# A 64x64 triangular inverse finished ahead of a four-group recurrence, one solve per group

## The chip, the cores and the metric

One core of one Trainium2 chip runs one program. The metric is the device time in microseconds (us) of one execution; the median of three runs of the kernel before is 899.11 us (898.23 to 902.22). Differences below 0.5% (4.5 us) count as no change.

## The reference

A trunk of two residual layers over 256 tokens of width 1024 in float32. The first layer adds an RWKV-7 time mixing and a retention to the residual, the second a differential attention; each layer then has a cross-attention into 256 memory tokens and a squared-ReLU MLP. Only the RWKV-7 scan matters here. It is, per head (8 heads of 64 channels) and per token t:

```
sa    = state @ a_t
state = state * w_t + sa (x) b_t + v_t (x) k_t
y_t   = state @ r_t
```

with `a = -kk`, `b = kk * a`, decays `w`, and a state of 64x64 that starts at zero. Its output goes through a group norm, a gate and an output projection.

## The kernel before, in words

The scan is computed in chunks: the 256 tokens are four groups g of 64 tokens. Group g lies in half `hf = g // 2` (a half is 128 tokens, one per partition) and in the partitions `gg` of half `gp = g % 2` (0 to 63 or 64 to 127). Within a group the dependence of a token on earlier ones is a strictly lower triangular 64x64 matrix per head, so the group needs the inverse of a unit triangular matrix. `inverse()` (L573) computes on the vector engine only the two 32x32 diagonal blocks of that inverse, for 8 heads x 4 groups at once, and leaves them in `X` (128 x 16 x 32). The block between them is never formed: it is applied inside the recurrence, in three steps per group, with `ga` the first 32 tokens of a group and `gb` the last 32.

One pass of the loop over g (L749 on) is a chain:

- for g > 0, `RS = AR^T S` (L757 on): the state `S` of the group before, 8 matmuls of 64x64, four heads at a time (`h2` is the half of the partitions, that is the rows of the array, which holds the head's channels), each four followed by an addition into the right side `LV` on the vector engine (L763)
- `solve(ga)` (L766): 8 matmuls 32x32 by 64 columns, `LV` with `X`, and two copies out of the bank to `U`, columns 0 to 255 on DVE (L770) and 256 to 511 on ACT (L771)
- `Q` (L774 on): 8 matmuls 32x32 by 64 columns, `U` of `ga` with the scores `SCb`, and an addition into `LV` of `gb` (L778)
- `solve(gb)`: as `solve(ga)`
- for g < 3 the new state: 8 matmuls `kT, vT` into KVp, 8 matmuls `bT, U` into Sp, and vector operations with the decay (L792 to L797)

After g = 2 `outputs(0)` (L692), after the loop `finish(0)` (L727) and `outputs(1)`: outputs of a half are 32 matmuls of 64x64 (`U, SCb` and `vT, SCk`), the same product of `AR` with the state (8 or 16 matmuls, `YS`, in fours by `h2`), a group norm (reductions on DVE, a square on ACT, a power on POOL), four transposes and the gate.

All matmuls are written out in order by the program, but which one TensorE runs when is set by a scheduler that takes the instructions by priority as their inputs come free. Behind the recurrence stand the projections of the memory tokens for the cross-attention (`kv_chunk`, matmuls of `memh` and `meml` with the weights `hi` and `lo`, 128x128 by 256 or 512 columns, called filler below); they need nothing of the recurrence, and the scheduler puts them between its steps. Each engine then runs its list in that order and waits where an input is missing.

Matmul outputs go to eight banks in three pools: `acc` (4), `mm` (2), `tr` (2). All steps of the recurrence took theirs from `tr` (`tr_t()`). A float32 matmul appears in the trace as two MATMUL rows and two LDWEIGHTS rows (8 matmuls of `solve` are 16 rows), a matmul on split weights as one. The helper `mm` (L121) records nearly all matmuls, so groups are told apart by their tiles: `tr<-LV,X` is a solve, `tr<-U,SCb` at 32*32 is Q, `tr<-S,AR` is RS or YS, `tr<-vT,kT` is KVp, `tr<-U,bT` is Sp, and `mm<-memh,hi` and its like are filler. In a row, 32*32 or 64*64 is the part of the array that is used.

Of the kernel before, what the change touches and what calls it, by code (L numbers as in the profile page):

```python
# [37 lines left out]
def kernel(ctx: ExitStack, tc: tile.TileContext, ins: dict, out: bass.AP):  # L38
    nc = tc.nc
# [6 lines left out]
    const = ctx.enter_context(tc.tile_pool(name="const", bufs=1))  # L46
# [25 lines left out]
    def acc_t():  # L72
        return ps_acc.tile([128, 512], F32, tag="acc", name=nm("acc"))
# [45 lines left out]
    def mm(o, lhsT, rhs, start, stop):  # L119

        ins = nc.tensor.matmul(o, lhsT=lhsT, rhs=rhs, start=start, stop=stop)  # L121
        key = o.tensor.name
        prev = last_in_bank.get(key)
        if prev is not None:
            behind(ins, prev, "one accumulation group per bank")
        last_in_bank[key] = ins
# [56 lines left out]
    def proj_rows(w, c0, xT, evac, alloc):  # L183

        xh, xl = xT
        ps = [alloc(), alloc()]
        for pc in range(4):
            wh, wl = wpiece(w[pc * 256:(pc + 1) * 256, c0:c0 + 512].rearrange("(kt p) c -> p kt c", p=128), 2, 512)
            for t in range(2):
                for k2 in range(2):  # L190
                    kt = 2 * pc + k2
                    mm3_x(ps[t], xh[:, kt, t * 128:(t + 1) * 128], xl[:, kt, t * 128:(t + 1) * 128],
                          wh[:, k2, :], wl[:, k2, :], kt == 0, kt == 7)
        for t in range(2):
            evac(ps[t], t)
# [163 lines left out]
    omu = const.tile([128, 14], F32, name="omu")  # L359
    behind(nc.vector.tensor_scalar(omu, prm[:, R_MU:R_MU + 14], -1.0, 1.0, op0=ALU.mult, op1=ALU.add), d1[1], "the activations first")  # L360
    oka = const.tile([128, 4], F32, name="oka")
    const.tile([128, 22], F32, name="pad")

    quad = const.tile([128, 2], F32, name="quad")
    for q in range(4):
# [166 lines left out]
    def rope_evac(i):  # L532
        def ev(ps, t):
            p4 = ps.rearrange("p (h x d) -> p h x d", h=8, x=2)
            cs, sn = rope_tabs(i, t)
            dst = qkR[i][:, t, :].rearrange("p (h x d) -> p h x d", h=8, x=2)
            tm = scratch()[:, :512].rearrange("p (h x d) -> p h x d", h=8, x=2)
            nc.vector.tensor_tensor(dst, p4, cs.unsqueeze(2).broadcast_to([128, 8, 2, 32]), op=ALU.mult)
            for x in range(2):
                nc.vector.scalar_tensor_tensor(tm[:, :, x, :], p4[:, :, 1 - x, :], 2.0 * x - 1.0, sn,  # L540
                                               op0=ALU.mult, op1=ALU.mult)
            nc.vector.tensor_tensor(dst, dst, tm, op=ALU.add)
        return ev
# [30 lines left out]
    def inverse():  # L574
# [21 lines left out]
        nc.vector.transpose(X.rearrange("p h (m par) -> p m par h", par=2), Xc.rearrange("p s m -> p m s"))  # L596
        Xt[0] = X

    proj_rows(wh_in, A_COLS + 512, xT, rope_evac(1), acc_t)
    proj_rows(wh_in, A_COLS, xT, rope_evac(0), acc_t)  # L600
    kTr = to_chan(1)
# [74 lines left out]
    def hidx(hd):  # L676
        return (hd % 2) * 4 + hd // 2
# [12 lines left out]
    ycs = {}  # L690

    def outputs(hf):  # L692
        Yp = tr_t()
        for hd in range(8):
            for gp in range(2):
                gg = slice(gp * 64, gp * 64 + 64)
                e = slice(hd * 64, hd * 64 + 64)
                mm(Yp[gg, e], lhsT=SCb[gg, hf, hidx(hd), 64:128], rhs=U[gg, hf, e], start=True, stop=False)
                mm(Yp[gg, e], lhsT=SCk[gg, hf, hidx(hd), 64:128], rhs=vT[gg, hf, e], start=False, stop=True)
        Y = pC.tile([128, 512], F32, tag="RH", name=nm("Y"))  # L700
        nc.scalar.activation(Y, Yp, AF.Copy)
        yg = slice(64, 128) if hf == 0 else slice(0, 128)
        for h2 in range(2):
            pr = slice(h2 * 64, h2 * 64 + 64)
            YS = tr_t()[:, :256].rearrange("p (b e) -> p b e", b=4)
            for gp in range(2):
                g = 2 * hf + gp
                gg = slice(gp * 64, gp * 64 + 64)
                if g > 0:
                    for b in range(4):  # L710
                        mm(YS[gg, b, :], lhsT=AR[pr, b * 4 + g, 1, :], rhs=Sv[g][pr, b, :], start=True, stop=True)
            yv = Y[yg, :].rearrange("p (b h e) -> p h b e", b=4, h=2)[:, h2]
            nc.vector.tensor_tensor(yv, YS[yg], yv, op=ALU.add)
        Y3 = Y.rearrange("p (h e) -> p h e", h=8)
        sm = small.tile([128, 8], F32, tag="sm8", name=nm("sm"))
        nc.vector.tensor_reduce(sm, Y3, axis=AX.X, op=ALU.add, negate=True)
        nc.vector.tensor_scalar(sm, sm, 1.0 / 64, None, op0=ALU.mult)
        yc = pC.tile([128, 8, 64], F32, tag="yc", name=nm("yc"), bufs=2)
        nc.vector.tensor_tensor(yc, Y3, sm.unsqueeze(2).broadcast_to([128, 8, 64]), op=ALU.add)
        sq = pC.tile([128, 8, 64], F32, tag="ysq", name=nm("ysq"))  # L720
        nc.scalar.activation(sq, yc, AF.Square)
        s2 = small.tile([128, 8], F32, tag="s28", name=nm("s2"))
        nc.vector.tensor_reduce(s2, sq, axis=AX.X, op=ALU.add)
        rs = rstd_of(s2, 64, 8, GN_EPS)
        nc.vector.tensor_tensor(yc, yc, rs.unsqueeze(2).broadcast_to([128, 8, 64]), op=ALU.mult)
        ycs[hf] = yc

    def finish(hf):
# [14 lines left out]
        nc.vector.tensor_tensor(ya, ya, pg2.rearrange("p (b t) -> p b t", b=4), op=ALU.mult)  # L743
        split(yT[0][:, 0:4, hf * 128:(hf + 1) * 128], yT[1][:, 0:4, hf * 128:(hf + 1) * 128], ya)


    U = pA.tile([128, 2, 512], F32, tag="bt", name="U")
    Sv = [None]
    for g in range(4):  # L749
        hf, gp = g // 2, g % 2  # L750
        ga = slice(gp * 64, gp * 64 + 32)
        gb = slice(gp * 64 + 32, gp * 64 + 64)
        gg = slice(gp * 64, gp * 64 + 64)
        S = Sv[g]
        RH = LV[:, hf, :]
        if g > 0:
            for h2 in range(2):  # L757
                RS = tr_t()[:, :256].rearrange("p (b e) -> p b e", b=4)
                pr = slice(h2 * 64, h2 * 64 + 64)
                for b in range(4):  # L760
                    mm(RS[gg, b, :], lhsT=AR[pr, b * 4 + g, 0, :], rhs=S[pr, b, :], start=True, stop=True)
                rv = RH[gg, :].rearrange("p (b h e) -> p h b e", b=4, h=2)[:, h2]
                nc.vector.tensor_tensor(rv, RS[gg], rv, op=ALU.add)  # L763
        Up = tr_t()

        def solve(prt):  # L766
            for hd in range(8):
                e = slice(hd * 64, hd * 64 + 64)
                mm(Up[prt, e], lhsT=Xt[0][prt, hf * 8 + hidx(hd), :], rhs=RH[prt, e], start=True, stop=True)
            nc.vector.tensor_copy(out=U[prt, hf, 0:256], in_=Up[prt, 0:256])  # L770
            nc.scalar.activation(U[prt, hf, 256:512], Up[prt, 256:512], AF.Copy)  # L771

        solve(ga)
        Q = tr_t()  # L774
        for hd in range(8):
            e = slice(hd * 64, hd * 64 + 64)
            mm(Q[gb, e], lhsT=SCb[ga, hf, hidx(hd), 32:64], rhs=U[ga, hf, e], start=True, stop=True)
        nc.vector.tensor_tensor(RH[gb, :], Q[gb, :], RH[gb, :], op=ALU.add)  # L778
        solve(gb)
        if g < 3:  # L780
            KVp, Sp = (tr_t()[:, :256].rearrange("p (b e) -> p b e", b=4) for _ in range(2))
            for tgt, lh, rh in ((KVp, kT, vT), (Sp, bT, U)):
                for hd in range(8):
                    b, h2 = hd // 2, hd % 2
                    e = slice(hd * 64, hd * 64 + 64)
                    mm(tgt[h2 * 64:h2 * 64 + 64, b, :], lhsT=lh[gg, hf, e], rhs=rh[gg, hf, e], start=True, stop=True)
            Sn = pC.tile([128, 4, 64], F32, tag="S", name=nm("S"), bufs=3)
            SP = pC.tile([128, 4, 64], F32, tag="SP", name=nm("SP"), bufs=1)

            pg = Ep.rearrange("p (b g) t -> p b g t", b=4)[:, :, g, 64:65]  # L790
            if g == 0:
                nc.vector.tensor_tensor(SP, KVp, pg.broadcast_to([128, 4, 64]), op=ALU.mult)  # L792
            else:
                nc.vector.tensor_tensor(SP, KVp, S, op=ALU.add)
                nc.vector.tensor_tensor(SP, SP, pg.broadcast_to([128, 4, 64]), op=ALU.mult)
            for b in range(4):
                nc.vector.scalar_tensor_tensor(Sn[:, b, :], Sp[:, b, :], pg[:, b, :], SP[:, b, :], op0=ALU.mult, op1=ALU.add)  # L797
            Sv.append(Sn)
        if g == 2:
            outputs(0)  # L800
# [505 lines left out]
```

## Time and profile before

| what | value |
|---|---|
| median of three runs | 899.11 us (898.23 to 902.22) |
| the profiled execution, device time | 897.66 us |
| its span in the profile | 895.9 us |
| PE busy (matmul) | 876.5 us, 98% |
| DVE, ACT busy | 593.5 us, 454.9 us |
| granted TensorE clock, mean | 0.995 |
| the recurrence with its outputs | about 153 to 214 us of the span |

The span is the time from the first to the last instruction; the device time is 1.8 us more. PE busy counts a matmul from its start to its modelled end, so rows of matmuls overlap; what a run of matmuls costs TensorE is read from the start of its first row to the start of the next work.

### The profile page before, as it was taken

The page shows a single profiled execution, that of the slowest core. Times are in us where ns is not written, and L with a number is a line of the kernel's source. Part 1 is how long each engine was busy: PE and PEld are TensorE (multiplying, and loading weights), DVE is VectorE, ACT ScalarE, POOL GpSimd, SP SyncE. Part 2 cuts the span into 40 slices and gives each one's busy share as a digit, 9 for nine tenths or more (in the row PEclk, how much of TensorE's full clock was granted, in tenths as well). Part 3 has the DMA queues.
Part 4 walks back from the last instruction along what each step waited for, and adds up shares of the span by engine and source line. Part 5 has one row for each costly group of instructions (what it writes and reads, how often), then busy time and mean ns, then how long its engine had stood idle before and what let it go on. Part 6 is the DMA issues. An engine that isn't in the chain of part 4 may idle for free.

```text
span 895.9 us, 14122 instructions
## 1 busy us (share of the span) xinstructions
PE 876.5 (98%) x5546; PEld 752.6 (84%) x5546; DVE 593.5 (66%) x937; ACT 454.9 (51%) x730; POOL 30.5 (3%) x51
## 2 busy tenths in 40 slices
PE   7999999999999999999999999999999999999996
PEld 5988889777889889888888889978899888888885
DVE  4669888455476557666666675786776676666665
ACT  5765444324465436444444454674564554444443
POOL 2000000001000100000000000001000000000001
PEclk8999999999999999999999999999999999999999
DMA  9754433222656545565555555443563465655551
GB/s 310 237 152 129 140 120 119 72 72 95 198 203 213 185 168 191 195 190 192 193 189 189 188 175 180 142 124 113 170 203 97 153 198 188 188 189 191 188 189 66
DMA packets 47078, 149.98 MB, mean 167 GB/s; under 512 B 4731, under 2 KB 4900, under 8 KB 46884
## 3 DMA queue, kind: packets, MB, share of 16 engines
q1 hardware_dynamic: 45456, 142.73, 49.2%
q10 hardware_dynamic: 1108, 3.72, 1.2%
q0 software_dynamic: 448, 2.63, 0.8%
q8 instruction: 43, 0.70, 0.3%
q14 instruction: 23, 0.19, 0.1%
HBM read 148.01 MB, written 2.63 MB: 168 GB/s over the span
## 4 chain that ended last, share of the span: by engine, by line
PE 90%; DVE 4%; issue 2%; ACT 2%; POOL 1%; DMA 1%; POOLq 0%; SPq 0%; DVEq 0%; ACTq 0%
PE mm L121 37%; PE acc L121 35%; PE tr L121 15%; DVE lo L129 1%; PE tr L254 1%; ACT hi L129 1%; DMA h<-in_x_dram 1%; PE tr L1111 1%; PE tr L958 1%; DVE z L1092 0%; PE acc L254 0%; POOL rs L226 0%; DVE xn L268 0%; PE tr L500 0%; POOL xn L1189 0%
## 5 line engine op out<-in xcount | busy, mean ns | idle before, releaser
L129 DVE TENSOR_TENSOR lo<-raw,hi 128x1024 fp32r<-128x1024 f32 x262 | 320.0, 1223 | 213.3 <-ACT hi L129 211.1
L129 ACT ACTIVATE hi<-raw 128x1024 fp32r<-128x1024 f32 x262 | 277.6, 1060 | 333.5 <-PE mm L121 122.5
L121 PE MATMUL mm<-xhl,hi 128*128 128x256 f32 (+1 forms) x784 | 188.0, 319 | 1.3 <-ACT xhl L129 1.1
L121 PEld LDWEIGHTS mm<-xhl,hi 128*128 128x128 f32 x784 | 129.7, 189 | 12.1 <-ACT xhl L129 2.0
L121 PE MATMUL mm<-xhl,lo 128*128 128x256 f32 x512 | 138.1, 282 | 0.0
L121 PE MATMUL acc<-hi,hl 128*128 128x512 f32 x256 | 100.2, 391 | 0.0
L121 PE MATMUL acc<-hi,hh 128*128 128x512 f32 x256 | 100.1, 391 | 0.0
L121 PE MATMUL acc<-lo,hh 128*128 128x512 f32 x256 | 99.6, 389 | 0.0
L121 PEld LDWEIGHTS mm<-xhl,lo 128*128 128x128 f32 x512 | 96.6, 189 | 2.5
L121 PE MATMUL tr<-xhl,hi 128*128 128x512 f32 x256 | 92.8, 395 | 0.0
L121 PE MATMUL acc<-hi,xhl 128*128 128x512 f32 x256 | 81.9, 396 | 0.0
L121 PE MATMUL tr<-xhl,lo 128*128 128x256 f32 x256 | 66.7, 281 | 0.0
L121 PEld LDWEIGHTS acc<-hi,hl 128*128 128x128 f32 x256 | 48.0, 188 | 11.3 <-DVE hl L129 0.9
L121 PEld LDWEIGHTS acc<-lo,hh 128*128 128x128 f32 x256 | 48.1, 188 | 10.4
L121 PEld LDWEIGHTS acc<-hi,xhl 128*128 128x128 f32 x256 | 47.7, 188 | 9.7
L121 PEld LDWEIGHTS acc<-hi,hh 128*128 128x128 f32 x256 | 48.1, 188 | 8.8
L121 PEld LDWEIGHTS tr<-xhl,hi 128*128 128x128 f32 x256 | 48.2, 188 | 8.5
L121 PEld LDWEIGHTS tr<-xhl,lo 128*128 128x128 f32 x256 | 48.2, 188 | 2.9
L121 PE MATMUL acc<-lo,xhl 128*128 128x512 f32 x128 | 50.4, 394 | 0.0
L121 PE MATMUL mm<-memh,hi 128*128 128x256 f32 x128 | 37.0, 289 | 0.0
L121 PE MATMUL mm<-meml,hi 128*128 128x256 f32 x128 | 36.8, 288 | 0.0
L121 PE MATMUL mm<-memh,lo 128*128 128x256 f32 x128 | 36.5, 285 | 0.0
(303 smaller groups left out, 1369.5 us busy)
## 6 DMA issues: line engine op xcount, KB each, us to landing
raw<-in_w_dram SPq DMA_DIRECT2D x64, 512.0 KB, 4.3
raw<-in_mlp_w_dram SPq DMA_DIRECT2D x64, 512.0 KB, 4.3
raw<-in_hyb_w_in_dram SPq DMA_DIRECT2D x16, 512.0 KB, 3.7
raw<-in_w_k_dram SPq DMA_DIRECT2D x16, 512.0 KB, 3.5
raw<-in_xattn_w_kv_dram SPq DMA_DIRECT2D x16, 512.0 KB, 3.7
raw<-in_w_q_dram SPq DMA_DIRECT2D x16, 512.0 KB, 4.0
raw<-in_xattn_w_o_dram SPq DMA_DIRECT2D x16, 512.0 KB, 3.5
raw<-in_w_dqk_dram SPq DMA_DIRECT2D x16, 512.0 KB, 3.6
```

What stands on the lines that cost most here:

```text
L121: ins = nc.tensor.matmul(o, lhsT=lhsT, rhs=rhs, start=start, stop=stop)
L129: return nc.scalar.activation(hi, src, AF.Copy), nc.vector.tensor_tensor(lo, src, r32(hi), op=ALU.subtract)
L254: nc.tensor.transpose(ps[:, k4, :], x[:, kt * 128:(kt + 1) * 128], ident)
L958: nc.tensor.transpose(pt[:, j, m, :], P[:, j, m * 128:(m + 1) * 128], ident)
L1111: nc.tensor.transpose(pt[:, k * 128:(k + 1) * 128], z3[:, 0, k * 128:(k + 1) * 128], ident)
```

## The change

The whole 64x64 inverse is formed once, ahead of the loop, by the new function `whole_inverse()`: `T` (128 x 16 x 64) gets the two diagonal blocks from `X`, and its third block from two sets of 32 matmuls of 32x32 by 32 columns (scores with the transposed blocks, then the result with the blocks). Two activations, one 32x32-block transpose on DVE, and four copies out of banks (two on ACT, two on DVE, by half of the partitions) go with it. In the loop `solve(ga)`, `Q` and `solve(gb)` become one solve: 8 matmuls of 64x64 by 64 columns, four heads into the partitions `gg` of one bank and four into the other partitions `og` of a second bank, in turn. RS and YS alternate the two row halves `h2`, with a bank for each. RS, the solve and the outputs take their banks from `acc` instead of `tr`.

```diff
+    def whole_inverse():
+
+        X = Xt[0]
+        T = pB.tile([128, 16, 64], F32, tag="Lc", name="T")
+        for j in range(2):
+            nc.scalar.activation(T[:, :, j * 32:j * 32 + 32], X, AF.Identity, scale=quad[:, j:j + 1])
+        Xn = pB.tile([128, 16, 32], F32, tag="Xc", name="Xn")
+        nc.vector.transpose(Xn.rearrange("p h t -> p (h t)"), X.rearrange("p h t -> p (h t)"))
+        Wt = pC.tile([128, 16, 32], F32, tag="ysq", name="Wt")
+        Wp, Tp = (acc_t().rearrange("p (h t) -> p h t", h=16) for _ in range(2))
+        quads = [(slice(gp * 64, gp * 64 + 32), slice(gp * 64 + 32, gp * 64 + 64)) for gp in range(2)]
+        for i in range(16):
+            for ga, gb in quads:
+                mm(Wp[gb, i, :], lhsT=SCb[ga, i // 8, i % 8, 32:64], rhs=Xn[ga, i, :], start=True, stop=True)
+        nc.scalar.activation(Wt[quads[0][1]], Wp[quads[0][1]], AF.Copy)
+        nc.vector.tensor_copy(out=Wt[quads[1][1]], in_=Wp[quads[1][1]])
+        for i in range(16):
+            for ga, gb in quads:
+                mm(Tp[ga, i, :], lhsT=Wt[gb, i, :], rhs=X[gb, i, :], start=True, stop=True)
+        nc.scalar.activation(T[quads[0][0], :, 32:64], Tp[quads[0][0]], AF.Copy)
+        nc.vector.tensor_copy(out=T[quads[1][0], :, 32:64], in_=Tp[quads[1][0]])
+        Xt[0] = T
...
     def outputs(hf):
-        Yp = tr_t()
+        Yp = acc_t()
...
-        for h2 in range(2):
-            pr = slice(h2 * 64, h2 * 64 + 64)
-            YS = tr_t()[:, :256].rearrange("p (b e) -> p b e", b=4)
+        YS = [tr_t()[:, :256].rearrange("p (b e) -> p b e", b=4) for _ in range(2)]
+        for b in range(4):
             for gp in range(2):
                 g = 2 * hf + gp
                 gg = slice(gp * 64, gp * 64 + 64)
-                if g > 0:
-                    for b in range(4):
-                        mm(YS[gg, b, :], lhsT=AR[pr, b * 4 + g, 1, :], rhs=Sv[g][pr, b, :], start=True, stop=True)
+                for h2 in range(2 if g > 0 else 0):
+                    pr = slice(h2 * 64, h2 * 64 + 64)
+                    mm(YS[h2][gg, b, :], lhsT=AR[pr, b * 4 + g, 1, :], rhs=Sv[g][pr, b, :], start=True, stop=True)
...
+    whole_inverse()
...
         if g > 0:
+            RS = [acc_t()[:, :256].rearrange("p (b e) -> p b e", b=4) for _ in range(2)]
+            for b in range(4):
+                for h2 in range(2):
+                    pr = slice(h2 * 64, h2 * 64 + 64)
+                    mm(RS[h2][gg, b, :], lhsT=AR[pr, b * 4 + g, 0, :], rhs=S[pr, b, :], start=True, stop=True)
...
-        solve(ga)
-        Q = tr_t()
-        for hd in range(8):
-            e = slice(hd * 64, hd * 64 + 64)
-            mm(Q[gb, e], lhsT=SCb[ga, hf, hidx(hd), 32:64], rhs=U[ga, hf, e], start=True, stop=True)
-        nc.vector.tensor_tensor(RH[gb, :], Q[gb, :], RH[gb, :], op=ALU.add)
-        solve(gb)
+        Up = [acc_t()[:, :256] for _ in range(2)]
+        for hd in range(4):
+            for x in range(2):
+                e = slice((4 * x + hd) * 64, (4 * x + hd) * 64 + 64)
+                mm(Up[x][(gg, og)[x], hd * 64:hd * 64 + 64], lhsT=Xt[0][gg, hf * 8 + hidx(4 * x + hd), :], rhs=RH[gg, e],
+                   start=True, stop=True)
+        nc.vector.tensor_copy(out=U[gg, hf, 0:256], in_=Up[0][gg])
+        nc.scalar.activation(U[gg, hf, 256:512], Up[1][og], AF.Copy)
```

One more line shortens an unused `pad` tile by six columns; the `solve` function is gone.

The scheduler's order shows three places. The first is TensorE's list ahead of the first solve. `tr_1517` and `tr_1535` are the two halves of `LV`, `tr_1642` is KVp of g = 0, `mm_2066` is filler.

```order
 L121 MATMUL tr_1517<-vT_801,SCk 64x64 x16
 L121 MATMUL tr_1535<-vT_801,SCk 64x64 x16
-L121 MATMUL tr_1554<-LV,X 32x64 x8
+L121 MATMUL acc_1559<-Xn,SCb 32x32 x32
+L121 MATMUL tr_1642<-vT_801,kT_827 64x64 x8
+L121 MATMUL mm_2066<-meml,hi_2098 128x256
+L121 MATMUL mm_2066<-memh,lo_2099 128x256
+L121 MATMUL acc_1560<-X,Wt 32x32
```

Where the first `solve(ga)` stood, the first set of the third block (`Xn, SCb`) now stands, then KVp of g = 0 and the start of the second set (`X, Wt`).

The second place is TensorE's list behind the second solve. `tr_1692` is Sp of g = 1, `tr_1741` is KVp of g = 2, `acc_1717` and `acc_1718` are the two banks of RS of g = 2.

```order
-L121 MATMUL tr_1622<-LV,X 32x64
+L121 MATMUL tr_1692<-U,bT_814 64x64 x8
+L121 MATMUL tr_1741<-vT_801,kT_827 64x64 x8
+L121 MATMUL mm_2128<-meml,hi_2160 128x256
+L121 MATMUL mm_2128<-memh,lo_2161 128x256
+L121 MATMUL mm_2128<-memh,hi_2160 128x256
+L121 MATMUL acc_1717<-S_1709,AR 64x64
+L121 MATMUL acc_1718<-S_1709,AR 64x64
```

At this depth of the filler the kernel before was inside its solve of g = 1; the change has left g = 1 and begins RS of g = 2, the two row halves in turn. From the `LV` matmuls to the last YS the list before has 36 runs of recurrence work with filler between (56 matmuls of 256 columns and 72 of 512), the list of the change 19 runs (56 and 22).

The third place is DVE's list at the same point as the first.

```order
 L570 TENSOR_TENSOR SCk<-tr_1476,prm 128x512
+L606 STREAM_TRANSPOSE Xn<-X 128x512
 L570 TENSOR_TENSOR SCk<-tr_1486,prm 128x512
 L570 TENSOR_TENSOR SCk<-tr_1496,prm 128x512
 L570 TENSOR_TENSOR SCk<-tr_1506,prm 128x512
-L770 COPY U<-tr_1554 32x256
-L778 TENSOR_TENSOR LV<-tr_1565,LV 32x512
+L809 TENSOR_TENSOR SP_1661<-tr_1642,Ep 128x256
+L614 COPY Wt<-acc_1559 32x512
```

The transpose of `X` now stands ahead of three of the four copies of the masked scores `SCk`. On every engine the order outside this stretch is as before.

## Rows read from the trace of the kernel before

**Rows 1.** The page, its first part: busy time, share of the span, instructions.

```profile
PE 876.5 (98%) x5546; PEld 752.6 (84%) x5546; DVE 593.5 (66%) x937; ACT 454.9 (51%) x730; POOL 30.5 (3%) x51
```

**Rows 2.** Windows: us, PE, PEld, DVE, ACT, POOL busy (instructions), PEclk, DMA share, GB/s.

```profile
8.00:10.00 2.00, 0.27 (x2) 0.27 (x3) 1.35 (x4) 0.77 (x3) 1.14 (x2) 0.82 1.05 392
10.00:12.00 2.00, 2.00 (x11) 2.00 (x11) 2.00 (x4) 0.86 (x2) 0.08 (x1) 0.50 1.02 412
...
150.00:215.00 65.00, 64.71 (x775) 50.11 (x774) 33.11 (x61) 19.86 (x31) 1.64 (x1) 1.00 0.23 75
```

**Rows 3.** Groups by shape, PE: form, count, busy us, mean ns, idle before.

```profile
L121 PE MATMUL tr<-LV,X 32*32 32x64 f32 x128 | 9.2, 216 | 0.0
L121 PE MATMUL tr<-S,AR 64*64 64x64 f32 x96 | 7.4, 226 | 0.0
...
L121 PE MATMUL tr<-U,SCb 32*32 32x64 f32 x64 | 5.0, 217 | 0.0
```

**Rows 4.** Timeline of PE, 187 to 190 us: start, us, instruction, count.

```profile
187.06 0.40 PE L121 MATMUL mm<-hi,memh 128*128 128x512 f32 x1
187.29 0.39 PE L121 MATMUL mm<-lo,memh 128*128 128x512 f32 x1
187.61 1.08 PE L121 MATMUL tr<-LV,X 32*32 32x64 f32 x16
188.62 0.68 PE L121 MATMUL tr<-vT,kT 64*64 64x64 f32 x16
189.23 0.50 PE L121 MATMUL mm<-hi,meml 128*128 128x512 f32 x1
189.57 0.40 PE L121 MATMUL mm<-hi,memh 128*128 128x512 f32 x1
```

**Rows 5.** Timeline of PE, one half of Q and the filler behind it.

```profile
157.05 0.63 PE L121 MATMUL tr<-U,SCb 32*32 32x64 f32 x8
157.61 0.39 PE L121 MATMUL mm<-memh,hi 128*128 128x256 f32 x1
```

**Rows 6.** Timeline of PE, S,AR matmuls of outputs(0) and of outputs(1).

```profile
192.86 0.68 PE L121 MATMUL tr<-S,AR 64*64 64x64 f32 x8
193.46 0.51 PE L121 MATMUL mm<-hi,meml 128*128 128x512 f32 x1
...
211.51 0.92 PE L121 MATMUL tr<-S,AR 64*64 64x64 f32 x16
212.35 0.51 PE L121 MATMUL mm<-hi,meml 128*128 128x512 f32 x1
```

**Rows 7.** Timeline of PE, the matmuls of LV, both halves of the array in turn.

```profile
153.13 2.21 PE L121 MATMUL tr<-vT,SCk 64*64 64x64 f32 x61
```

**Rows 8.** Timeline of PE, layer 2: score matmuls that alternate two row halves.

```profile
552.81 0.28 PE L121 MATMUL mm<-xhl,hi 128*128 128x256 f32 x1
552.93 0.28 PE L121 MATMUL mm<-xhl,lo 128*128 128x256 f32 x1
553.14 1.58 PE L121 MATMUL acc<-kTd,qTd 64*128 64x128 f32 x16
554.65 0.50 PE L121 MATMUL mm<-xhl,hi 128*128 128x256 f32 x2
```

**Rows 9.** Timeline of DVE ahead of the recurrence.

```profile
146.97 1.20 DVE L596 STREAM_TRANSPOSE X<-Xc 128x512 f32<-128x512 f32 x1
...
149.88 0.68 DVE L570 TENSOR_TENSOR SCk<-tr,prm 128x512 f32<-128x512 f32 x1
151.55 1.29 DVE L570 TENSOR_TENSOR SCk<-tr,prm 128x512 f32<-128x512 f32 x2 [0.99 <-PE tr L121]
```

**Rows 10.** Timeline of DVE: the first copy of U, and the group norm's last step.

```profile
156.38 0.41 DVE L770 COPY U<-tr 32x256 f32<-32x256 f32 x1 [2.25 <-PE tr L121]
...
205.86 0.69 DVE L725 TENSOR_TENSOR yc<-yc,rs 128x512 f32<-128x512 f32 x1 [1.75 <-POOL rs L226]
```

**Rows 11.** Timeline of ACT: the other copy of U.

```profile
156.88 0.37 ACT L771 ACTIVATE U<-tr 32x256 f32<-32x256 f32 x1 [0.90 <-DVE U L770]
```

More of the change, by code (lines that the diff above doesn't have):

```diff
@@ L361 @@
     oka = const.tile([128, 4], F32, name="oka")
-    const.tile([128, 22], F32, name="pad")
+    const.tile([128, 16], F32, name="pad")
     quad = const.tile([128, 2], F32, name="quad")
@@ L708, in outputs @@
                 gg = slice(gp * 64, gp * 64 + 64)
[L709 to L711 removed]
+                for h2 in range(2 if g > 0 else 0):
+                    pr = slice(h2 * 64, h2 * 64 + 64)
+                    mm(YS[h2][gg, b, :], lhsT=AR[pr, b * 4 + g, 1, :], rhs=Sv[g][pr, b, :], start=True, stop=True)
+        for h2 in range(2):
             yv = Y[yg, :].rearrange("p (b h e) -> p h b e", b=4, h=2)[:, h2]
[L713 removed]
+            nc.vector.tensor_tensor(yv, YS[h2][yg], yv, op=ALU.add)
         Y3 = Y.rearrange("p (h e) -> p h e", h=8)
@@ L750 @@
         hf, gp = g // 2, g % 2
-        ga = slice(gp * 64, gp * 64 + 32)
-        gb = slice(gp * 64 + 32, gp * 64 + 64)
         gg = slice(gp * 64, gp * 64 + 64)
+        og = slice(64 - gp * 64, 128 - gp * 64)
         S = Sv[g]
@@ L756 @@
         if g > 0:
+            RS = [acc_t()[:, :256].rearrange("p (b e) -> p b e", b=4) for _ in range(2)]
+            for b in range(4):
+                for h2 in range(2):
+                    pr = slice(h2 * 64, h2 * 64 + 64)
+                    mm(RS[h2][gg, b, :], lhsT=AR[pr, b * 4 + g, 0, :], rhs=S[pr, b, :], start=True, stop=True)
             for h2 in range(2):
[L758 to L761, printed above, removed]
                 rv = RH[gg, :].rearrange("p (b h e) -> p h b e", b=4, h=2)[:, h2]
-                nc.vector.tensor_tensor(rv, RS[gg], rv, op=ALU.add)
-        Up = tr_t()
-        def solve(prt):
-            for hd in range(8):
-                e = slice(hd * 64, hd * 64 + 64)
-                mm(Up[prt, e], lhsT=Xt[0][prt, hf * 8 + hidx(hd), :], rhs=RH[prt, e], start=True, stop=True)
-            nc.vector.tensor_copy(out=U[prt, hf, 0:256], in_=Up[prt, 0:256])
-            nc.scalar.activation(U[prt, hf, 256:512], Up[prt, 256:512], AF.Copy)
-        solve(ga)
-        Q = tr_t()
-        for hd in range(8):
-            e = slice(hd * 64, hd * 64 + 64)
-            mm(Q[gb, e], lhsT=SCb[ga, hf, hidx(hd), 32:64], rhs=U[ga, hf, e], start=True, stop=True)
-        nc.vector.tensor_tensor(RH[gb, :], Q[gb, :], RH[gb, :], op=ALU.add)
-        solve(gb)
+                nc.vector.tensor_tensor(rv, RS[h2][gg], rv, op=ALU.add)
+        Up = [acc_t()[:, :256] for _ in range(2)]
[6 more added lines that the diff above has]
+        nc.scalar.activation(U[gg, hf, 256:512], Up[1][og], AF.Copy)
         if g < 3:
```

## The prediction

> **What bounds the kernel now.** First the page's busy times: PE is busy for 98% of the span [rows 1], so the first question is whether the recurrence, a chain of small steps, leaves TensorE waiting at all. The windows answer it: from 150 to 215 us, the LV matmuls and the whole recurrence with its outputs, PE is busy for 64.71 of 65 us at a granted clock of 1.00, with the DMA engines at 0.23 [rows 2]. The latency of the chain is covered by filler, and shortening the chain is worth nothing in itself. What counts is how much TensorE time the recurrence takes from the filler. So the reader should look at groups by shape, and at the timeline of PE from the start of one run to the start of what follows.
>
> The shapes show 128 rows of solves and 64 of Q, all on a 32x32 corner of the array, and 96 of `S,AR` [rows 3]. What a run costs depends on whether successive matmuls use the same part of the array:
>
> - same part: 16 rows of a solve take 188.62 - 187.61 = 1.01 us [rows 4], 8 rows of Q 0.56 [rows 5], 8 rows of S,AR at 64x64 0.60 [rows 6]; about 0.063 to 0.075 a row
> - parts in turn: 16 rows of `vT,kT`, same row half and the two column halves in turn, 0.61 [rows 4]; the LV matmuls, both halves in turn, (2.21 less a matmul's own 0.22) / 60 = 0.033 a row [rows 7]
> - two row halves in turn under all columns: 16 rows of `kTd,qTd`, half of them 256 and half 128 columns, 1.51 us [rows 8]. With 0.12 for a filler matmul of 256 columns [rows 8] and half that for 128, streaming alone would be 8 x 0.12 + 8 x 0.06 = 1.44. Hardly anything of the weight loads is left to see.
>
> Each change between filler and small matmuls costs too. Filler matmuls of 512 columns follow each other in 0.23; the one ahead of a run takes 0.32, the one behind it 0.34 [rows 4]: 0.09 + 0.11, say 0.19 a run.
>
> **The change, part by part** (TensorE time, since that ends the stretch).
>
> Removed: per group two solves of 1.01 and two half Qs of 0.56 [rows 4, 5], 3.14; for four groups 12.6 us.
>
> Added, solves: 8 matmuls with one row half and two column halves in turn. That is the pattern of `vT,kT`, 0.61 [rows 4], so 4 x 0.61 = 2.4. If they ran like one part it would be twice 0.60 each [rows 6], 4.8. I take 2.4, since rows and columns of the array are used exactly as in the nearer row.
>
> The Trainium skill says otherwise of this pattern: in "TensorE: Matmul & The Clock Gate", section "What overlaps and what doesn't", a weight load overlaps a running matmul only where the row group differs. By that rule `vT,kT` at 0.61 should cost about 1.2, and the trace does not agree; by the rule the solves would cost 4.8 and the result would be 2.4 us later.
>
> Added, third block: 64 matmuls of 32x32 by 32 columns, 128 rows, the two 64-partition halves in turn. No row has 32 columns. Upper end: one part, 1.01 / 16 x 128 = 8.1 [rows 4]. Lower end: half of the alternating price, as the columns are half, 2.2. I take the alternating price itself, 128 x 0.033 = 4.3 [rows 7], since alternation is what the code writes and nothing here shows that fewer columns are cheaper.
>
> Moved, S,AR: before, six runs of 8 rows for RS and two for outputs(0) at 0.60, and two of 16 for outputs(1) at 0.84 [rows 6]: 6.5 us. After, six runs of 16 rows. Row halves in turn hid the loads in [rows 8], so I take 0.61 each as for `vT,kT`: 3.7, a gain of 2.8. The lower end is no gain.
>
> Fewer runs: 36 become 19, 17 x 0.19 = 3.2 [rows 4].
>
> Sum on PE: 12.6 - 2.4 - 4.3 + 2.8 + 3.2 = 11.9 us less.
>
> New waits. Less filler between steps means that PE may reach a step before its input.
>
> - The transpose for `Xn`, 1.20, stands on DVE behind the first SCk copy. That ends at 150.56 and DVE then idled 0.99 [rows 9]; so the next copy starts some 0.25 late, and with it the score matmuls that wait for its bank: 0.3.
> - Handover of U. DVE starts its copy 0.1 behind the solve and takes 0.41 [rows 10]; before, ACT's copy began only after DVE's, at 156.88 [rows 11]. Now each reads a bank of its own, so both are done after some 0.6. Behind them wait four matmuls of Sp for DVE's half and four for ACT's. The cover is 5 and 4 filler matmuls (0.8, 0.7 with the change of shape) and, for g = 2, ten output matmuls. The two LV additions behind RS need 0.6 and 1.05, covered by 7, 6 and 5 filler matmuls and a first pair of solves. It is tight, but covered; 0.4 in all.
> - The transposes of finish(0) want `yc`, the end of four DVE passes like the one at 205.86 (0.69 each, with a wait of 1.75 for POOL [rows 10]) and a square on ACT, 5 us or so, behind a weight split on the same queue. The cover is the last solve, 30 output matmuls and 13 of filler, about 5.5: 0.4, and as much again for YS of outputs(1), which waits for the gate's bank.
>
> Together 1.5. Copies of `Wt` and `T` lie beside KVp and filler and cost nothing; without that cover they would be 0.7 each. Banks in `acc`: each is taken again four allocations later, and its reader is done by then by these sums.
>
> Behind the recurrence 50 matmuls of 512 columns that were between its steps now follow it. Their number is the same, DMA has room (0.23), so they cost what they did.
>
> Net 11.9 - 1.5 = 10.4. The profiled execution took 897.66, which gives 887.3; its distance to the median of the runs, 899.11, is 1.45, so the forecast is **888.7 us**, 1.2% faster. (Below 0.5%, 4.5 us, a measurement of this kernel can't tell a difference from none.)
>
> **The rivals.**
>
> - *The parts do not run side by side.* Third block at 8.1, solves at 4.8, S,AR with no gain: 3.8 + 2.4 + 2.8 = 9.0 less gain, 897.7, no change. For it: no row has 32 columns, or two row halves into the same columns at 64 wide. Against: every row in which parts take turns is cheap [rows 4, 7, 8]. All three: 6%; one of the three, 891 to 893: 12%.
> - *Waits take the place of the filler.* PE's list is fixed; 78 filler matmuls now lie within the stretch where 128 lay, and a late DVE step holds all behind it. With 0.5 more at each of some ten handovers, 894. For it: the additions are covered by tenths. Against: the copies now run in parallel. 8%.
> - *The chain was the point, and its work is not what costs.* If small matmuls took time that PE would otherwise have lost anyway (waiting for split weights), the time stays near 899. Against: filler keeps 0.12 and 0.23 between the runs, and DMA is at 0.23. 5%.
> - *Slower: the clock falls.* At 8 to 10 us PE did almost nothing, 0.27 of 2 us, and from 10 to 12 the granted clock was 0.50 [rows 2], the lower of the two levels, 1.2 GHz of 2.4. Ahead of the first solve some 8 us now hold small matmuls alone, and fewer filler matmuls follow among the next ones. If the lower level came and stayed through the stretch, the filler in it (56 x 0.12 + 22 x 0.23 = 11.8) would double and the small matmuls (some 26 us) lengthen by up to as much, half of it 13: 888.7 + 24.8 = 913.5. It decides once more than about 10 us are lost, that is 20 us of PE work at that level. Against: before, 5.9 us of small matmuls with no filler but seven ran at 1.00 [rows 2]. 4%.
>
> **How the numbers follow.** The forecast's own case (887 to 891) has 65%, one part not overlapping 12%, waits 8%, all three 6%, nothing gained 5%, the clock 4%. Faster by over 0.5% (below 894.6): 65 + 12 + 8 = 85%; no change: 6 + 5 = 11%; slower 4%. The range: at the low end the third block at 2.2 (2.1 less) and no new waits (1.5 less), 885.1; at the high end the waits' case and one part with no overlap, 894.5. That leaves out 15% and the tails of the cases inside.
>
> **What would show it.** In the profile after, a solve of 8 matmuls should take 0.6 us with the two column halves in turn, the `X` and `Xn` groups 2.2 us each, S,AR runs of 8 matmuls 0.6; no `tr<-LV,X` or `tr<-U,SCb` at 32*32 should be left. PE should stay busy, with idle of some 1.5 us between 150 and 200, and the last YS should end some 22 us earlier (10 us gained, 12 of filler moved behind it). Wrong would be: PE waiting for `U` or `LV` for several us, a granted clock under 1.00 in the stretch, or runs of the third block over 4 us each.

## The result and the profile after

The changed kernel takes 885.54 us (median of four runs, 884.97 to 886.23) where the kernel before, on the same chip, takes 898.67 (898.04 to 902.22): a ratio of 0.9848, interval 0.9824 to 0.9872. It is 13.1 us faster; the forecast was 10.4. Executions of one and the same kernel lie about 1.1 us apart by how soon the clock is up at the program's start (mean granted clock 0.991 or 0.994), so sizes below 1 us are read from the stretch of the recurrence in the profile and not from medians.

The page of the changed kernel, its first part, answers to [rows 1]:

```profile
PE 864.1 (98%) x5546; PEld 746.8 (84%) x5546; DVE 590.8 (67%) x932; ACT 455.3 (51%) x730; POOL 30.3 (3%) x51
```

TensorE was the bound and still is; it has 12.4 us less to do with the same number of instructions. A window over the stretch, with the columns of [rows 2]:

```profile
150.00:195.00 45.00, 43.30 (x753) 36.38 (x750) 28.23 (x57) 15.36 (x27) 1.64 (x1) 1.00 0.22 71
```

The clock stayed at 1.00; 1.7 us of 45 are idle. The groups by shape, as [rows 3]:

```profile
L121 PE MATMUL acc<-LV,T 64*64 64x64 f32 x64 | 3.4, 228 | 0.0
L121 PE MATMUL acc<-S,AR 64*64 64x64 f32 x48 | 2.9, 235 | 0.1
...
L121 PE MATMUL tr<-S,AR 64*64 64x64 f32 x48 | 2.2, 225 | 0.0
...
L121 PE MATMUL acc<-X,Wt 32*32 32x32 f32 x64 | 1.4, 192 | 0.0
L121 PE MATMUL acc<-Xn,SCb 32*32 32x32 f32 x64 | 1.2, 192 | 0.0
```

The 192 rows of solves and Q at 32*32 are gone; 64 rows of solves at 64*64 and 128 short rows of the third block stand in their place. The timeline of PE through the third block and the first solve (start, us, instruction, count):

```profile
156.69 1.20 PE L121 MATMUL acc<-Xn,SCb 32*32 32x32 f32 x64
157.82 0.68 PE L121 MATMUL tr<-vT,kT 64*64 64x64 f32 x16
158.43 0.39 PE L121 MATMUL mm<-meml,hi 128*128 128x256 f32 x1
158.66 0.28 PE L121 MATMUL mm<-memh,lo 128*128 128x256 f32 x1
158.86 0.24 PE L121 MATMUL acc<-X,Wt 32*32 32x32 f32 x2
159.04 0.39 PE L121 MATMUL mm<-memh,hi 128*128 128x256 f32 x1
...
160.18 1.19 PE L121 MATMUL acc<-X,Wt 32*32 32x32 f32 x62
161.30 0.39 PE L121 MATMUL mm<-memh,lo 128*128 128x256 f32 x1
...
162.22 0.68 PE L121 MATMUL acc<-LV,T 64*64 64x64 f32 x16
162.83 0.39 PE L121 MATMUL mm<-memh,lo 128*128 128x256 f32 x1
```

From start to start, the first set costs 157.82 - 156.69 = 1.13 us for 64 rows, 0.018 a row; the second 0.18 + 1.12 (two rows, filler, 62 rows). That is 2.4 in all. The solve costs 162.83 - 162.22 = 0.61.

**Where the time went.** From the first LV matmul to the work behind the last YS the trace has 60.78 us before (152.90 to 213.68) and 36.95 after (154.32 to 191.27). Filler in it, at 0.118 and 0.2345 us a piece, is 56 + 72 pieces before (23.5) and 56 + 22 after (11.8). What is left is the recurrence's own: 37.3 before, 25.2 after, **12.1 less**, of which one wait of 1.26 is already taken off. Ahead of the stretch the profiled execution lost 1.4 at its slower start; behind it, with the filler that moved there taken off, the program is 0.7 shorter, of which some 0.6 is the line on `pad` (experiment 7).

### The profile page after: what moved, and what is told of

It reads as the page before. It is cut to its first block, busy times and chain, and to the rows that moved or that the text cites. A ratio compares the mean times of both kernels' runs of the same rounds, so it can differ in the third digit from the quotient of the medians.

```text
span 884.5 us, 14111 instructions
## 1 busy us (share of the span) xinstructions
PE 864.1 (98%) x5546; PEld 746.8 (84%) x5546; DVE 590.8 (67%) x932; ACT 455.3 (51%) x730; POOL 30.3 (3%) x51
## 4 chain that ended last, share of the span: by engine, by line
PE 88%; DVE 5%; issue 3%; ACT 2%; POOL 1%; DMA 1%; POOLq 0%; SPq 0%; DVEq 0%; ACTq 0%
PE acc L121 36%; PE mm L121 36%; PE tr L121 13%; DVE lo L129 1%; ACT hi L129 1%; PE tr L254 1%; POOL rs L226 1%; DMA h<-in_x_dram 1%; PE tr L1128 1%; PE tr L975 1%; DVE z L1109 0%; PE acc L254 0%; DVE xn L268 0%; PE tr L500 0%; POOL xn L1206 0%
## 5 line engine op out<-in xcount | busy, mean ns | idle before, releaser
L121 PEld LDWEIGHTS mm<-xhl,hi 128*128 128x128 f32 x784 | 129.7, 189 | 11.8 <-ACT xhl L129 1.7
L121 PEld LDWEIGHTS acc<-lo,hh 128*128 128x128 f32 x256 | 48.1, 188 | 10.4
```

## The experiments

All are compared with the kernel before, run in between; differences to the changed kernel are those of the ratios, times 899. "Own" is the stretch less its filler, as above. The intervals are 1.6 to 4.3 us wide, so ratios do not tell apart changed kernels that differ by less than some 2 us; there "own" decides.

| kernel | median us | ratio, interval | to the changed kernel | own us |
|---|---|---|---|---|
| changed kernel | 885.54 | 0.9848, 0.9824 to 0.9872 | 0 | 25.2 |
| 1 row turns alone | 897.96 | 0.9986, 0.9977 to 0.9995 | before: -1.3 | 36.5 |
| 2 no row turns | 886.62 | 0.9862, 0.9849 to 0.9876 | +1.3 | 26.2 |
| 3 one column half | 887.48 | 0.9867, 0.9853 to 0.9882 | +1.7 | 26.0 |
| 4 third block by half | 894.83 | 0.9959, 0.9946 to 0.9973 | +10.0 | clock fell |
| 5 transposing banks | 890.75 | 0.9910, 0.9895 to 0.9925 | +5.6 | 29.4 |
| 6 longer chain | 885.68 | 0.9849, 0.9833 to 0.9866 | +0.1 | 24.9 |
| 7 pad as before | 886.27 | 0.9860, 0.9845 to 0.9875 | +1.1 | 25.2 |
| 8 finish(0) later | 882.85 | 0.9822, 0.9808 to 0.9837 | -2.3 | 19.0 |
| 9 first set by half | 885.37 | 0.9850, 0.9830 to 0.9871 | +0.2 | 26.1 |
| 10 second set by half | 893.49 | 0.9937, 0.9920 to 0.9954 | +8.0 | clock fell |
| 11 solves on old banks | 886.49 | 0.9857, 0.9837 to 0.9876 | +0.8 | 26.4 |
| 12 in fours | 886.65 | 0.9858, 0.9835 to 0.9880 | +0.9 | 25.8 |
| 13 second set, filler kept | 886.14 | 0.9863, 0.9848 to 0.9878 | +1.3 | 26.0 |
| 14 both sets, filler kept | 887.93 | 0.9875, 0.9858 to 0.9891 | +2.4 | 26.9 |

(Kernel 8's own time is without finish(0) and without most output matmuls of half 1, which both stand behind the last YS there.)

### 1. The row turns alone, in the kernel before

```diff
+            RS = [tr_t()[:, :256].rearrange("p (b e) -> p b e", b=4) for _ in range(2)]
+            for b in range(4):
+                for h2 in range(2):
...
-                RS = tr_t()[:, :256].rearrange("p (b e) -> p b e", b=4)
-                for b in range(4):
```

> The kernel before with one part of the change alone: RS and YS take the two row halves in turn, with a bank of tr for each; solves, Q and the rest as before. Theory (TensorE's own time for the runs counts, the chain is covered): S,AR runs of 8 matmuls fall from 1.2 us to 0.61, six of them, 2.8 us less in the stretch, so 895.9 against 898.7. Rival (the latency of the chain counts): three RS steps lie in the chain, each 0.6 shorter, but the second addition now waits for both halves: 1 us less or none, 898. Rival (two row halves into the same columns do not overlap): runs stay at 1.2, no change.

Less than half of it came: 1.3 us by the ratio, 0.8 in the stretch. With only the two `tr` banks the second bank of a pair is not free when the first is, and the scheduler takes four matmuls of one row half and then four of the other. Only in outputs(1) do the halves alternate. The turns need the banks.

### 2. The changed kernel without row turns

```diff
-            for b in range(4):
-                for h2 in range(2):
+            for h2 in range(2):
+                for b in range(4):
```

(and the same in outputs)

> The changed kernel with RS and YS in fours by row half again (banks and solves as in the change). Theory: six S,AR runs go from 0.61 back to 1.2 us, less what a wait of PE absorbs: 885.5 + 2.8 = 888.3. Rival (row halves in turn do not overlap): no change, 885.5. Rival (latency counts): up to 1.8 more for three RS steps, 887.3, with PE idle in front of the additions.

1.3 us by the ratio, 1.0 in the stretch, of which 0.2 is a longer wait for `yc` (1.48 instead of 1.26). The two runs of YS in outputs(1) went from 0.61 to 0.89; RS of g = 1 costs the same in either form, since in the changed kernel too it runs in four pairs between filler, as the columns of `S` come in. So the order of the rows is worth 1, not 2.8; where `S` comes in pieces, the second bank alone makes the pairs.

### 3. Both halves of a solve in the same partitions

```diff
-                mm(Up[x][(gg, og)[x], hd * 64:hd * 64 + 64], lhsT=Xt[0][gg, hf * 8 + hidx(4 * x + hd), :], rhs=RH[gg, e],
+                mm(Up[x][gg, hd * 64:hd * 64 + 64], lhsT=Xt[0][gg, hf * 8 + hidx(4 * x + hd), :], rhs=RH[gg, e],
```

> The changed kernel with both bank halves of the solve written into the same partitions, so that all 8 matmuls of a solve use the same quarter of the array. Theory (columns in turn hide the weight load): a solve goes from 0.61 to 1.2 us, four of them, 2.4 more, 887.9. Rival (only another row group hides it, as a page of the notes says): a solve is the same in both forms, 885.5.

The first solve in its timeline of PE:

```profile
162.34 1.14 PE L121 MATMUL acc<-LV,T 64*64 64x64 f32 x16
163.41 0.38 PE L121 MATMUL mm<-memh,lo 128*128 128x256 f32 x1
```

163.41 - 162.34 = 1.07 against 0.61: 0.46 for this solve, and 1.6 over the four by their rows. By the ratio the kernel is 1.7 longer; in the stretch 0.8, since the wait for `yc` fell from 1.26 to 0.68 and RS of g = 2 takes 0.2 less. The weight rows lie in the same row half in both kernels; only the column half differs. In the single records of the trace, the two column halves of a pair start 0.007 us apart in the changed kernel and pairs follow each other in 0.058; here single rows follow each other in 0.058. Two halves run side by side, a pair in the time of one row.

The Trainium skill's rule ("TensorE: Matmul & The Clock Gate", section "The mechanism", under "What overlaps and what doesn't") is that weights load beside a running matmul only where the row group differs. Read as in the prediction, it would make the two kernels equal; the measurement decides against that reading. It does not decide against the rule: two halves that load together and then run together give the same spacing, and no run here shows a load beside a matmul of the same row half.

### 4. The third block by half

```diff
-        for i in range(16):
-            for ga, gb in quads:
+        for ga, gb in quads:
+            for i in range(16):
```

(both sets)

> The changed kernel with the third block's two sets of 32 matmuls ordered by partition half (16 of one corner of the array, then 16 of the other) instead of in turn. In the changed kernel's trace a set takes 1.13 us, 0.018 a row, half of the forecast. Theory A (they are cheap because the two halves take turns): in one corner a row costs about 0.05 to 0.06, a set 3.2 to 4, together 4.2 to 5.5 more, 890 to 891. Theory B (they are cheap because 32 columns are few): a set stays near 1.1 to 1.3 us, 885.5 to 886.

Neither theory has 10 us. The first set took 2.03 us, 0.032 a row, at full clock: above theory B's 1.1 to 1.3 and well under theory A's 3.2 to 4. Then the clock fell. The first set in the timeline of PE, and windows of this kernel, columns as above:

```profile
154.91 2.11 PE L121 MATMUL acc<-Xn,SCb 32*32 32x32 f32 x64
156.94 0.68 PE L121 MATMUL tr<-vT,kT 64*64 64x64 f32 x16
```

```profile
158.00:160.00 2.00, 2.00 (x59) 2.00 (x59) 0.79 (x2) 0.00 (x0) 0.00 (x0) 0.83 0.00 0
160.00:178.00 18.00, 18.00 (x165) 14.78 (x163) 6.53 (x15) 4.06 (x6) 0.00 (x0) 0.50 0.09 31
```

For some 20 us TensorE was granted 0.50, the lower of its two levels, though it was busy all the time. So the clock rival of the prediction is real, one order of a loop away from the changed kernel. Experiments 9, 10 and 12 to 14 ask what kept it off.

### 5. The banks taken away

```diff
-        Yp = acc_t()
+        Yp = tr_t()
...
-            RS = [acc_t()[:, :256].rearrange("p (b e) -> p b e", b=4) for _ in range(2)]
+            RS = [tr_t()[:, :256].rearrange("p (b e) -> p b e", b=4) for _ in range(2)]
...
-        Up = [acc_t()[:, :256] for _ in range(2)]
+        Up = [tr_t()[:, :256] for _ in range(2)]
```

> The changed kernel with its extra banks taken away: Yp, RS and Up come from the two transposing banks again. Theory A (the banks let the short multiplications stand together: without them TensorE takes filler between the pieces of a solve or of RS, in about 29 runs instead of 17): 12 more runs of filler at 0.19 us and part of the row turns lost (0.3 to 1.5), so 2.5 to 4 us over the changed kernel, 888 to 890. Rival (the banks don't matter as long as there is filler): within 0.5 us of the changed kernel's 885.5. Rival (a solve that waits for a bank holds up the chain until filler runs out): over 892.

5.6 by the ratio, 4.2 in the stretch. RS of g = 1 in this kernel:

```profile
165.09 0.33 PE L121 MATMUL tr<-S,AR 64*64 64x64 f32 x2
165.34 0.39 PE L121 MATMUL mm<-memh,hi 128*128 128x256 f32 x1
165.56 0.28 PE L121 MATMUL mm<-meml,hi 128*128 128x256 f32 x1
165.77 0.33 PE L121 MATMUL tr<-S,AR 64*64 64x64 f32 x2
166.03 0.38 PE L121 MATMUL mm<-memh,lo 128*128 128x256 f32 x1
```

One matmul, filler, one matmul: a single one (two rows) between filler costs 166.03 - 165.77 = 0.26, as much as a pair in turn in the changed kernel, and the runs between filler go from 19 to 29. Ten more runs at 0.19 are 1.9 of the 4.2; the lost row turns are about as much again (RS of g = 2 takes 1.38 in four pieces instead of 0.84 in one). The chain held nothing up (beside the 0.29 for SCk, PE waits for nothing but `yc` here too). "More banks" is thus a third of the gain or more, and by way of short runs and lost turns, not of waits.

### 6. A longer chain

```diff
+        for _ in range(2):
+            nc.vector.tensor_scalar(RH[gg, :], RH[gg, :], 1.0, None, op0=ALU.mult)
         Up = [acc_t()[:, :256] for _ in range(2)]
```

> The changed kernel with two added VectorE passes over the right side of each group's solve (64 x 512, some 0.7 us each), which change no number: the chain of each group is some 1.4 us longer, 4 to 5.5 us over the four, and TensorE has no more work. Theory A (TensorE's work is what counts, the chain is covered by filler): at most 0.5 us more than the changed kernel, since the filler that covers it only moves; with 17 runs of filler as before. Rival (the gain came from a shorter chain, which is what ends the stretch): 4 to 5.5 us more, 889.5 to 891.

Nothing: +0.1. The stretch grew to 42.98 us, but with 27 more filler pieces in it (56 + 49); its own time is 24.9. The eight passes took 0.42 us each, 3.4 in all and not the 4 to 5.5 of the expectation, and PE waited for the longer chain once, 0.23 us. The chain of the recurrence is covered, with at least some 3 us to spare; what the change gained is TensorE work.

### 7. The pad

```diff
-    const.tile([128, 16], F32, name="pad")
+    const.tile([128, 22], F32, name="pad")
```

> The changed kernel with the unused pad tile as wide as it was (22 columns instead of 16). Theory A (the pad only shifts where tiles lie in memory): the changed kernel's time within 0.5 us, 885 to 886. Rival (0.7 us of the gain, seen in 512-column filler that comes every 0.231 instead of 0.2345 us, is where the tiles lie): 0.7 to 1.5 us more.

The rival, though at its lower end. The stretch is the same, 36.96; behind it the profiled execution takes 885.1 - 191.33 = 693.8 us instead of 884.5 - 191.27 = 693.2. By the ratio it is 1.1, but the intervals overlap. The traces settle it: the spacing of filler, which the expectation named, differs. Of the run of filler behind the last YS the first and the 146th matmul, in the changed kernel and in this one:

```profile
191.27 0.50 PE L121 MATMUL mm<-lo,memh 128*128 128x512 f32 x1
...
225.17 0.39 PE L121 MATMUL mm<-hi,meml 128*128 128x512 f32 x1
```

```profile
191.33 0.50 PE L121 MATMUL mm<-lo,memh 128*128 128x512 f32 x1
...
225.47 0.40 PE L121 MATMUL mm<-hi,meml 128*128 128x512 f32 x1
```

33.90 us become 34.14. Over all traces the median spacing of 512-column filler is 0.234 us in the three kernels with the wide pad (before, 1 and 7) and 0.231 to 0.232 in the thirteen with the narrow one. So some 0.6 us of the gain is the six columns of a tile that nothing reads, and no part of the inverse. Which tile's place does it was not tried.

### 8. finish(0) later

```diff
-    finish(0)
     outputs(1)
...
         kv_chunk(0, i, KT0, V0)
+        if i == 4:
+            finish(0)
```

> The changed kernel with finish(0) written after the fifth chunk of keys and values instead of ahead of them, so that its transposes stand behind more filler in the order. Theory A (the one new wait of the changed kernel is TensorE's 1.26 us for yc): this wait goes and nothing takes its place, 1.0 to 1.5 us less than the changed kernel, 884.0 to 884.5, ahead of both kernels. Rival (the wait only moves, to finish(1) or to the outputs behind it): within 0.4 us of the changed kernel.

Faster than both kernels: 882.22 to 883.62 in four runs, all below the changed kernel's lowest of 884.97. In its timeline of PE the transposes of finish(0) have no idle time ahead:

```profile
191.65 0.60 PE L757 MATMUL tr<-prm,yc 128*128 128x128 f32 x4
```

It gained 2.3 where 1.0 to 1.5 was expected: beside the wait of 1.26, YS of outputs(1) now stands against the last solve. Up to the last YS 14 runs are left of 19, but two more stand behind it (the output matmuls and finish(0)); three runs fewer are 3 x 0.19 = 0.6. The other 0.5 no row explains.

### 9 and 10. One set by half

The diff of experiment 4, in one of the two sets.

> The changed kernel with only the first set of the third block (SCb by Xn) ordered by half, one 32x32 corner at a time; the second set still takes the halves in turn. In the kernel with both sets by half the first took 2.03 us instead of 1.13 and the granted clock fell a few us behind it. Theory C1 (the first set alone, 2 us of one corner, lets the clock fall): 0.9 us for the set and 5 to 8 us for a stretch at the lower level, 891 to 894.5. Rival C2 (it takes both sets, 128 rows of one corner within 6 us): the clock stays at 1.00 and the cost is the set's own 0.9 us, 886 to 887.

> The changed kernel with only the second set of the third block (X by Wt) by half; the first takes the halves in turn. Theory C1 (2 us of one corner is enough, whichever set it is): 891 to 894.5 with a stretch at a granted clock of .50 behind 162 us. Rival C2 (both sets are needed): 886 to 887, clock 1.00. Rival C3 (it depends on what stands ahead: the LV multiplications and the first set, 1 us of filler, then this set; more filler ahead of it than ahead of the first set keeps the clock up here though not in the run with the first set by half): 886 to 887 here and 891 or more there.

With the first set slow the clock stays at 1.00 and the stretch is 0.9 us longer, as C2 has it (the median of 885.37 is below its 886 to 887); with the second set slow it falls, as C1 has it. So it does depend on what stands ahead, but the other way round than C3 said. The timeline of PE of the second kernel, and its windows:

```profile
156.10 1.20 PE L121 MATMUL acc<-Xn,SCb 32*32 32x32 f32 x64
157.23 0.68 PE L121 MATMUL tr<-vT,kT 64*64 64x64 f32 x16
157.84 0.39 PE L121 MATMUL mm<-meml,hi 128*128 128x256 f32 x1
158.07 0.28 PE L121 MATMUL mm<-memh,lo 128*128 128x256 f32 x1
158.28 2.11 PE L121 MATMUL acc<-X,Wt 32*32 32x32 f32 x64
160.31 0.39 PE L121 MATMUL mm<-memh,hi 128*128 128x256 f32 x1
```

```profile
155.00:160.00 5.00, 5.00 (x174) 4.69 (x173) 1.12 (x2) 1.78 (x3) 0.00 (x0) 1.00 0.02 3
160.00:165.00 5.00, 5.00 (x70) 4.38 (x68) 2.35 (x4) 2.63 (x4) 0.00 (x0) 0.60 0.01 3
165.00:170.00 5.00, 5.00 (x33) 3.52 (x30) 1.28 (x6) 0.00 (x0) 0.00 (x0) 0.50 0.30 105
...
180.00:185.00 5.00, 4.96 (x121) 4.60 (x122) 2.13 (x8) 0.67 (x2) 0.00 (x0) 0.85 0.06 23
```

But the two kernels differ in more than the set. In the kernel that lost the clock all 64 rows of the second set come in one piece, and the eight filler matmuls that stand in the changed kernel from 159.04 to 160.18 have gone from that place: by half, the first half's 32 rows need only ACT's copy of `Wt`, so the scheduler has no gap to fill. Turns or filler: that was open.

### 11. The solves alone on the old banks

Only the last part of experiment 5's diff.

> The changed kernel with the solves alone on the two transposing banks; Yp and RS keep their extra banks. With all three on the transposing banks it took 5.6 us more. In this order 23 runs stand between filler instead of 19 (the other kernel has 29). If the cost goes with the number of runs at 0.19 us: 0.8 us more than the changed kernel, 886 to 886.5. If it is the solves' banks that the whole cost hangs on: 889.5 to 891. If the banks of the solves don't matter: 885 to 885.7.

+0.8 by the ratio, 1.2 in the stretch, with 23 runs instead of 19: 0.2 to 0.3 a run, near the 0.19. The rest of experiment 5's cost, 3.0 of 4.2 in the stretch, lies with RS and the outputs.

### 12. In fours

```diff
-        for i in range(16):
-            for ga, gb in quads:
+        for i, (ga, gb) in [(i, q) for c in range(0, 16, 4) for q in quads for i in range(c, c + 4)]:
```

> The changed kernel with both sets of the third block ordered in fours: four heads of one half, then four of the other. A row cost 0.032 us in one corner and 0.018 with the halves in turn; if only the row at a change of corner is cheap, a set takes some 1.8 us instead of 1.13, 1.4 us more over both. [...] Rival D2 (changing corners every fourth head is enough to keep the clock): 886.3 to 887.3 with the clock at 1.00.

The clock stayed, and the first set took 1.43 us, 0.022 a row: less than was expected, so more than the one row at a change of corner is cheap. Here too filler stands between pieces of the second set.

### 13 and 14. By half, with the filler put back

```diff
-        for i in range(16):
-            for ga, gb in quads:
+        for i, (ga, gb) in [(0, q) for q in quads] + [(i, q) for q in quads for i in range(1, 16)]:
```

(the second set; in experiment 14 the first set is by half as well)

> The second set of the third block by half as in the run that lost the clock, but with the first head's two rows ahead, so that TensorE's order has the eight 256-column filler multiplications between that pair and the other 62 rows, as the changed kernel has; in the run that lost the clock they had dropped out of that place. Theory F (what keeps the clock is filler among the small multiplications): 1.00 throughout, and the cost is the set's price of 0.9 us, 885.8 to 887. Theory R (what keeps the clock is the halves in turn, that is the price of a row): the granted clock falls to .50 here too, 891 to 894.5.

> Both sets by half, with the same eight filler multiplications between the first pair of the second set and its other 62 rows. Theory F: the clock stays at 1.00 and the cost is twice 0.9 us, 886.8 to 888. Theory R: it falls, 891 to 895. If the run with the second set alone by half keeps the clock and this one doesn't, it takes both, and each alone is no answer.

Theory F, twice. The timeline of PE of kernel 13, and a window of kernel 14:

```profile
159.24 0.24 PE L121 MATMUL acc<-X,Wt 32*32 32x32 f32 x2
159.41 0.39 PE L121 MATMUL mm<-memh,hi 128*128 128x256 f32 x1
...
160.34 0.28 PE L121 MATMUL mm<-meml,hi 128*128 128x256 f32 x1
160.55 1.99 PE L121 MATMUL acc<-X,Wt 32*32 32x32 f32 x62
162.47 0.39 PE L121 MATMUL mm<-memh,lo 128*128 128x256 f32 x1
```

```profile
150.00:195.00 45.00, 43.12 (x748) 36.55 (x747) 26.76 (x56) 15.45 (x26) 1.64 (x1) 1.00 0.21 72
```

The rows of kernel 13 are as slow as those of kernel 10 (162.47 - 160.55 = 1.92 for 62), yet the clock holds, and the costs are those of the rows: 0.8 and 1.7 us in the stretch. Kernels 10 and 13 do the same matmuls and differ by where eight 256-column filler matmuls stand, about 1 us of work; that place is worth (0.9937 - 0.9863) x 899 = 6.7 us. The same holds for 4 and 14 (7.6). It is no matter of single executions: the mean granted clock is 0.980 to 0.984 in all ten of kernels 4 and 10, and 0.991 to 0.995 in all eight of 13 and 14. Whether the turns alone, without that filler, would have kept the clock was not tried.

## Why the prediction was right, and where it was wrong

- **What bounds the kernel**: TensorE work, not the chain. Right; experiment 6 shows it directly.
- **Solves**, 4 x 0.61: right where a solve runs whole (the first, 0.61), and for the pattern given, column halves in turn (experiment 3). The second runs in two pieces, 0.26 + 0.49, and the other two are mixed with output matmuls, so "4 x" was not measured as such.
- **Third block**, "128 x 0.033 = 4.3": the step that failed, a term mis-sized by 1.9 of the 2.7 us that the forecast of 10.4 fell short of 13.1. It measured 2.4, near the lower bound. The alternating price of [rows 7] belongs to matmuls of 64 columns; the sentence "nothing here shows that fewer columns are cheaper" set it too high. In one corner a row of 32 columns cost 0.032 (experiments 4, 9, 13) where one of 64 had cost 0.063 [rows 4], and in turn 0.018 against 0.033: at these sizes the price went with the columns in both patterns (in the second the tile is smaller too, 32x32 against 64x64).
- **S,AR**, a gain of 2.8: too high. RS of g = 1 in four pieces of some 0.26, RS of g = 2 at 0.84, the 32 rows of RS of g = 3 and outputs(0) at 1.27, and outputs(1) at 2 x 0.61 make 4.4, not 3.7: a gain of 2.1. The price of a run was right where the run was whole; that RS would run in pieces, since its `S` comes column by column, was overlooked, though the kernel before did it too. One piece of RS of g = 1 before, then one after, and RS of g = 2 after:

```profile
164.28 0.33 PE L121 MATMUL tr<-S,AR 64*64 64x64 f32 x2
164.53 0.39 PE L121 MATMUL mm<-memh,lo 128*128 128x256 f32 x1
```

```profile
166.08 0.33 PE L121 MATMUL acc<-S,AR 64*64 64x64 f32 x4
166.34 0.39 PE L121 MATMUL mm<-meml,hi 128*128 128x256 f32 x1
...
171.40 0.91 PE L121 MATMUL acc<-S,AR 64*64 64x64 f32 x16
172.24 0.39 PE L121 MATMUL mm<-meml,hi 128*128 128x256 f32 x1
```

- **New waits**, 1.5: the size came out at 1.3 by luck, the places did not. Three of the four waits did not come: the one for SCk is 0.29 as it was, and neither U nor the last YS waits. The whole sum is the one for `yc`, given 0.4. PE, then DVE, in the changed kernel:

```profile
186.75 0.66 PE L757 MATMUL tr<-prm,yc 128*128 128x128 f32 x4 [1.26 <-DVE yc L748]
```

```profile
180.57 1.23 DVE L129 TENSOR_TENSOR lo<-raw,hi 128x1024 fp32r<-128x1024 f32 x1
181.71 0.17 DVE L740 TENSOR_SCALAR sm<-sm 128x8 f32<-128x8 f32 x1
...
186.00 0.69 DVE L748 TENSOR_TENSOR yc<-yc,rs 128x512 f32<-128x512 f32 x1 [1.75 <-POOL rs L226]
```

  The weight split that the prediction had named stands within the group norm on DVE's queue and holds it for 1.23 us; POOL's power holds it for 1.75 more. Which of the two would have to go for the wait to go was not tried. The chain, "5 us or so", and its cover, "about 5.5", were each read to half a microsecond, and their difference was the answer.
- **The sum**: 11.9 of work became 13.4 (1.9 for the third block, less 0.7 for S,AR, and 0.3 that no row explains), less 1.3 of waits: 12.1, as the stretch shows. With some 0.6 behind it for the pad, which the prediction put at nothing, that is 12.7 of the 13.1 of the medians. The median of 885.5 lies at the lower end of the range of 885.1 to 894.5; by the ratio it is 0.9848 x 898.67 = 885.0, just outside. That end stood for the third block at 2.2 and no new waits. The first came, the second did not; that the time is so near that end all the same is in part the pad and the 0.3, which nothing in the prediction stands for.
- **The rivals**: parts that do not run side by side, and waits in place of filler, did not come. The clock's fall did not come either, but it was rightly suspected in "small matmuls alone, and fewer filler matmuls follow": experiments 4 and 10 have it. The changed kernel has not "some 8 us" of them ahead of the first solve but 4.1 in one piece, and 16 filler matmuls among the rest. Its price was overstated: the 24.8 us took the lower level for the whole stretch, while in experiments 4 and 10 the full clock came back after some 20 us, and the loss beyond the rows' own price was 7 to 8.

## What to carry to other kernels

Where a filled TensorE is the bound, cost small matmuls by the part of the array that each uses: neighbours in other column or row halves run side by side (here 16 rows in 0.61 us instead of 1.07 or 0.89), and here that took a bank for each, or the scheduler took them apart again. Read the place of the large matmuls among them as well as their number: the same work in another order lost 7 us to the clock. Where a shorter stretch uncovers a wait, look at what else stands on the queue of the engine that is waited for: here a weight split of 1.23 us stood in the group norm, and it was not moved alone.

## What was not expected of the hardware

The granted clock fell to 0.50 with TensorE busy for 5.00 of every 5.00 us, after the LV matmuls, 128 rows at 32*32, a run of KVp and only two filler matmuls, while the next few were running (experiment 10), and it came back some 20 us later, while the recurrence was still running. The Trainium skill ("TensorE: Matmul & The Clock Gate", section "HAM oscillation — how this bites in real kernels") tells of the clock falling where TensorE waits for transfers; here it waited for nothing. TensorE's last idle time ahead of the fall, 0.29 us for `SCk`, ended at 153.14, and the granted clock was still 1.00 from 155 to 160.
